# V differences of the prompt attention: formed by the projection stage and kept in DRAM, or formed in the attention from two loads per key block

## The chip, the cores and the metric

The kernel is one program on one core of a Trainium2 chip. The metric is device time in microseconds (us), the median of several executions. Names of engines are those of the profile: PE is the matmul engine (PEld its weight loads), DVE the vector engine, ACT the scalar engine, POOL the GpSimd engine, and SP the queue from which this kernel issues its DMAs. Each engine, and SP too, works its own instructions in the order in which they are written, so a waiting instruction holds up all that stand behind it there.

## The reference, cut to what matters

Two layers (DEPTH = 2) are applied to a prompt of 2048 tokens and to 8 short sample sequences. In each layer one projection gives u, z_s, q, k, v and z_a; u goes through a state-space branch (SSM), q, k and v through a stick-breaking attention of 8 heads of 64; both results are gated, joined, and sent through an output projection onto the residual. What the change touches is the prompt attention:

```
z = einsum('bqhd,bkhd->bhqk', q, k) * HEAD_DIM ** -0.5      # 2048 x 2048 for each head
mask = k_pos < q_pos                                        # strictly causal
after = exclusive sum, from the right, of -softplus(z)
a = exp(log_sigmoid(z) + after) where mask, else 0
o = einsum('bhqk,bkhd->bqhd', a, v)
```

With u[s] the product of sigmoid(-z) over the keys from s up to the query, a[s] is the difference of two neighbouring u. The sum over a[s] v[s] can therefore be written with u[s] and with differences of neighbouring rows of V. The kernel does that: it never forms a, and it multiplies u by (V[s-1] - V[s]), with V[-1] = 0, and adds one row of V for each query at the end.

## The kernel before

Work is laid out in tiles of 128 tokens. `project` makes one of the six column groups for half of the tiles: for the group v it takes, for each tile, 24 matmuls (L673 to L675) into a PSUM tile pm (two buffers), an ACT copy into an SBUF tile kn (L760, three buffers), a store of it to the output and one to the DRAM tensor v_d. Then it reads the same tile back from v_d, shifted by one row, into an x2 tile (two buffers, shared with other uses and shown as x by the profile), subtracts on POOL (L771), and stores the result to a second DRAM tensor, dv_d:

```
dv = e2("x2", [128, 512], bufs=2)
self.dma(dv, self.v_d[l][i * 128 - 1:i * 128 + 127, :])
gp.tensor_sub(dv, dv, cp)
self.dma(self.dv_d[l][i * 128:(i + 1) * 128, :], dv)
```

This happens 32 times: for 16 prompt tiles in each of two layers, eight at a time in four v stages. In the trace these stages lie at about 310 to 402 us, 840 to 900, 1718 to 1800 and 2313 to 2368.

`attn_prompt` loops over blocks of up to four query tiles (t0, nt), pairs of heads (hp) and key blocks of 512 (kc), from the last to the first. One turn of the kc loop is called a unit here; there are 96, 40 in layer 0 and 56 in layer 1. A unit loads a tile V1 (named V in the profile; two buffers) from dv_d, and K; PE multiplies Q and K into pz (L819, L820), ACT takes the sigmoid (L824), DVE runs the product along the keys (a scan, L826, tile u), PE transposes u in blocks (L836, tile pt), DVE copies one head's block to SBUF (L838, tile aT) and ACT the other's (L839), and PE multiplies aT by V1 into po (L842). At the end of a head pair DVE adds the row of V and multiplies by the gate (L851). The prompt attention of layer 0 runs from about 1025 to 1920 us, with the layer's output projection and the first half of the next layer's input projection in between; that of layer 1 from about 2480 to the end.

Beside the first v stage (320 to 400 us) runs a part of `ssm_mats(1)`: powers of the state matrix, a chain of DVE instructions (L444, L446, L447, L449, tiles T and t) each of which needs a POOL instruction (L445, L448), then sines and cosines on ACT (L414, L415) and products on DVE and POOL (L416 to L419). The next weights are split into a high part wH on ACT and a low part wL by `split` (L171, L172), for every second of them on POOL.

The order on each engine isn't written out by hand: the program is built with a scheduler that puts all instructions in order by a time model of its own, so an edit in one place can move instructions of others.

## Time and profile before

| | us |
|---|---|
| median of 3 runs | 3268.61 |
| lowest and highest of them | 3263.90 and 3268.92 |
| the profiled execution | 3266.1 |
| its span, first to last instruction | 3264.3 |
| PE busy | 3019.6 (93%) |
| DVE busy | 2228.8 (68%) |
| ACT busy | 1297.2 (40%) |
| POOL busy | 715.0 (22%), 468 instructions |
| mean granted clock of PE, 1 is full | 0.971 |

The table is read so: PE works in 93% of the span, so what remains are about 245 us in which it waits, and some stretches in which its clock is lowered. Busy shares are means over stages with different limits; which wait ends last has to be looked up in each stage. The profiled execution lies 2.5 us under the median of the runs.

### The profile page before, as it was taken

Reading aid. Unit: us, or ns where it says so; the run is one execution under the profiler, and the core shown is the slowest. Engines: PE = TensorE matmul, PEld = TensorE weight load, DVE = VectorE, ACT = ScalarE, POOL = GpSimd, SP = SyncE. Lnnn points to the kernel's source line nnn. Section 1 sums busy time; section 2 is a strip of 40 time slices with the busy share of each in tenths; the row PEclk is TensorE's granted clock in tenths of the full one; section 3 lists DMA queues with packets and bytes.
Section 4 is the critical chain, followed back from the end, with each engine's and each line's share of the span. In section 5 each row is a group of like instructions: output and inputs, shape, how many; then the busy total and the mean of one; then the engine's idle time right before and its main releaser. Section 6 shows DMA issues by size and latency. Waiting matters only on the chain. (4 is left out here: it accounts for less than half of the span.)

```text
span 3264.3 us, 47172 instructions
## 1 busy us (share of the span) xinstructions
PE 3019.6 (93%) x16902; PEld 2241.4 (69%) x16902; DVE 2228.8 (68%) x3885; ACT 1297.2 (40%) x2646; POOL 715.0 (22%) x468
## 2 busy tenths in 40 slices
PE   6978679899998999999999999989999899999998
PEld 4756577798767667667777785757789565666665
DVE  6699785667466776677895534376583989776865
ACT  5622225334342343465443324263343345343422
POOL 1155663102211022211021002222200202111210
PEclk8989899999999999999999999999999899999999
DMA  6645654565776974343344237437853846444642
GB/s 208 164 141 176 215 166 150 146 192 167 258 241 216 315 218 151 121 139 117 113 150 153 88 104 268 142 99 216 268 177 119 259 129 200 141 128 136 203 140 73
DMA packets 516100, 555.28 MB, mean 170 GB/s; under 512 B 87203, under 2 KB 369491, under 8 KB 515098
## 3 DMA queue, kind: packets, MB, share of 16 engines
q1 hardware_dynamic: 515866, 552.26, 53.9%
q8 instruction: 134, 2.20, 0.3%
q14 instruction: 100, 0.82, 0.1%
HBM read 378.12 MB, written 169.86 MB: 168 GB/s over the span
## 5 line engine op out<-in xcount | busy, mean ns | idle before, releaser
L826 DVE TENSOR_TENSOR_SCAN u<-u 128x512 f32<-128x512 f32 (+3 forms) x640 | 722.2, 1162 | 94.2 <-ACT u L824 90.7
L673 PE MATMUL pm<-wH,hH 128*128 128x512 f32 x1088 | 448.9, 414 | 38.4 <-ACT kn L760 18.9
L675 PE MATMUL pm<-wH,hL 128*128 128x512 f32 x1088 | 446.2, 410 | 10.6 <-POOL hL L649 6.0
L674 PE MATMUL pm<-wL,hH 128*128 128x512 f32 x1088 | 444.0, 408 | 9.9 <-DVE wL L172 8.0
L839 ACT COPY aT<-pt 128x512 f32<-128x512 f32 (+1 forms) x376 | 174.9, 469 | 595.3 <-PE pt L836 569.1
L836 PEld LDWEIGHTS pt<-ident,u 128*128 128x128 f32 x2176 | 242.1, 142 | 230.8 <-issue 194.1
L824 ACT ACTIVATE u<-pz 128x512 f32<-128x512 f32 (+3 forms) x640 | 320.7, 535 | 177.1 <-PE pz L822 61.3
L838 DVE COPY aT<-pt 128x512 f32<-128x512 f32 (+1 forms) x376 | 199.4, 533 | 253.8 <-PE pt L836 242.3
L836 PE MATMUL pt<-ident,u 128*128 128x128 f32 x2176 | 352.0, 285 | 12.9 <-DVE aT L838 9.3
L842 PE MATMUL po<-aT,V 128*64 128x512 f32 (+1 forms) x1504 | 317.7, 505 | 16.0 <-DVE aT L838 8.1
L819 PE MATMUL pz<-K,Q 128*128 128x512 f32 (+2 forms) x640 | 272.9, 427 | 6.1 <-ACT u L824 1.8
L726 PE MATMUL pm<-hH,wH 128*128 128x384 f32 (+1 forms) x768 | 258.9, 337 | 18.4 <-DVE kn L731 18.4
L673 PEld LDWEIGHTS pm<-wH,hH 128*128 128x128 f32 x1088 | 210.0, 193 | 90.2 <-ACT kn L760 20.4
L728 PE MATMUL pm<-hH,wL 128*128 128x384 f32 (+1 forms) x768 | 257.4, 336 | 10.2 <-POOL wL L172 10.2
L172 POOL TENSOR_TENSOR wL<-wr,wH 128x512 fp32r<-128x512 f32 x96 | 152.1, 1595 | 498.2 <-ACT wH L171 326.8
L727 PE MATMUL pm<-hL,wH 128*128 128x384 f32 (+1 forms) x768 | 257.8, 336 | 0.0
L675 PEld LDWEIGHTS pm<-wH,hL 128*128 128x128 f32 x1088 | 210.2, 193 | 66.2 <-POOL hL L649 10.6
L674 PEld LDWEIGHTS pm<-wL,hH 128*128 128x128 f32 x1088 | 210.2, 193 | 58.8 <-DVE wL L172 11.3
L820 PE MATMUL pz<-K,Q 128*128 128x512 f32 (+2 forms) x640 | 236.3, 370 | 0.0
L1241 PE MATMUL pm<-owH,mH 128*128 128x512 f32 x512 | 205.0, 402 | 2.1 <-ACT mH L171 1.2
L1242 PE MATMUL pm<-owL,mH 128*128 128x512 f32 x512 | 204.1, 399 | 3.1 <-DVE owL L172 3.1
L1243 PE MATMUL pm<-owH,mL 128*128 128x512 f32 x512 | 202.4, 396 | 0.0
(373 smaller groups left out, 5252.0 us busy)
## 6 DMA issues: line engine op xcount, KB each, us to landing
wr<-in_w_in_dram SPq DMA_DIRECT2D x192, 256.0 KB
K<-kT SPq DMA_DIRECT2D x184, 256.0 KB
Q<-qT SPq DMA_DIRECT2D x112, 256.0 KB
wm<-in_w_mod_dram SPq DMA_DIRECT2D x24, 1024.0 KB
V<-dv_d SPq DMA_DIRECT2D x92, 256.0 KB
out_dram<-kn SPq DMA_DIRECT2D x68, 256.0 KB
qT<-x SPq DMA_DIRECT2D x64, 256.0 KB
kT<-x SPq DMA_DIRECT2D x64, 256.0 KB
```

The costliest lines, as they stand in the source:

```text
L673: pe.matmul(ps, hH[:, k, cs], wH[k], start=k == 0, stop=False)
L674: pe.matmul(ps, hH[:, k, cs], wL[k], start=False, stop=False)
L675: pe.matmul(ps, hL[:, k, cs], wH[k], start=False, stop=k == KT - 1)
L726: pe.matmul(ps[:, 0:n], wH[k][:, ws], hH[:, k, 0:n], start=k == 0, stop=False)
L727: pe.matmul(ps[:, 0:n], wH[k][:, ws], hL[:, k, 0:n], start=False, stop=False)
L728: pe.matmul(ps[:, 0:n], wL[k][:, ws], hH[:, k, 0:n], start=False, stop=k == KT - 1)
L819: pe.matmul(pz[:, c0:512], Q1[:, qi], K1[:, 0:N], start=True, stop=False)
L820: pe.matmul(pz[:, c0:512], Q2[:, qi], K1[:, 0:N], start=False, stop=not diag)
L824: sc.activation(u[:, o:512], pz[:, c0:c1], AF.Sigmoid, scale=-0.125)
L826: v.tensor_tensor_scan(un, un, un, 1.0 if diag else carry[hh * 4 + i], ALU.mult, ALU.bypass)
L836: pe.transpose(pTs[hh][:, i * 128:(i + 1) * 128], As[hh][i][:, off + j * 128:off + (j + 1) * 128], ident)
L842: mm = pe.matmul(po[c, s], V1[:, j, c], aTs[hh][:, s], start=diag and j == 0, stop=kc == 0 and j == 3, tile_position=(0, hh * 64))
```

## The change

`dv_d` is gone, with the read-back, the subtraction and the store in `project`. In `attn_prompt` each unit loads the plain rows of V from v_d into V1 and the rows one above into a new tile Vp (one buffer), and POOL subtracts in place. For the first key block (kc = 0, 36 of the 96 units) the row above does not exist; there a memset and two loads stand for one.

```
--- before.py
+++ after.py
-        self.dv_d = per([SEQ, 512], F32, "dv_d")
@@ project, after the store to v_d
-                        if i < 16:
-                            dv = e2("x2", [128, 512], bufs=2)
-                            if i == 0:
-                                gp.memset(dv[0:1, :], 0.0)
-                                self.dma(dv[1:128, :], self.v_d[l][0:127, :])
-                            else:
-                                self.dma(dv, self.v_d[l][i * 128 - 1:i * 128 + 127, :])
-                            gp.tensor_sub(dv, dv, cp)
-                            self.dma(self.dv_d[l][i * 128:(i + 1) * 128, :], dv)
@@ attn_prompt, in the kc loop
                     V1 = ap.tile([128, 4, 128], F32, name="V1", bufs=2)
-                    self.dma(V1[:, 0:nk // 128], self.dv_d[l][ks, rp].rearrange("(b p) c -> p b c", p=128))
+                    Vp = ap.tile([128, 4, 128], F32, name="Vp", bufs=1)
+                    nb = nk // 128
+                    self.dma(V1[:, 0:nb], self.v_d[l][ks, rp].rearrange("(b p) c -> p b c", p=128))
+                    if kc:
+                        self.dma(Vp[:, 0:nb], self.v_d[l][kc * 512 - 1:kc * 512 + nk - 1, rp].rearrange("(b p) c -> p b c", p=128))
+                    else:
+                        gp.memset(Vp[0:1, 0, :], 0.0)
+                        self.dma(Vp[1:128, 0, :], self.v_d[l][0:127, rp])
+                        self.dma(Vp[:, 1:nb], self.v_d[l][127:nk - 1, rp].rearrange("(b p) c -> p b c", p=128))
+                    gp.tensor_sub(V1[:, 0:nb], Vp[:, 0:nb], V1[:, 0:nb])
```

Lines behind the edit in `scratch` are one lower in the changed kernel (L771 has no successor; L760 is L759, L445 is L444, L172 is L171), those in `attn_prompt` behind the new loads are one lower too.

POOL in the first v stage, before (x_3710, x_3744, x_3777 and x_3810 are the differences of the first four tiles, t and T the power chain, kn in L698 the last k tile):

```order
L445 TENSOR_TENSOR t_2345<-T 128x16x32
L771 TENSOR_TENSOR x_3710<-x_3710,kn 128x512
L445 TENSOR_TENSOR t_2408<-T 128x16x32
L448 TENSOR_TENSOR t_2345<-T 128x16x32
L698 TENSOR_TENSOR kn<-kn,kg 128x512
L771 TENSOR_TENSOR x_3744<-x_3744,kn 128x512
L448 TENSOR_TENSOR t_2408<-T 128x16x32
L445 TENSOR_TENSOR t_2345<-T 128x16x63
L771 TENSOR_TENSOR x_3777<-x_3777,kn 128x512
L445 TENSOR_TENSOR t_2408<-T 128x16x63
L448 TENSOR_TENSOR t_2345<-T 128x16x63
L771 TENSOR_TENSOR x_3810<-x_3810,kn 128x512
```

and the same place of POOL in the changed kernel:

```order
L444 TENSOR_TENSOR t_2343<-T 128x16x32
L444 TENSOR_TENSOR t_2406<-T 128x16x32
L447 TENSOR_TENSOR t_2343<-T 128x16x32
L697 TENSOR_TENSOR kn<-kn,kg 128x512
L447 TENSOR_TENSOR t_2406<-T 128x16x32
L444 TENSOR_TENSOR t_2343<-T 128x16x63
L444 TENSOR_TENSOR t_2406<-T 128x16x63
L447 TENSOR_TENSOR t_2343<-T 128x16x63
L447 TENSOR_TENSOR t_2406<-T 128x16x63
L418 TENSOR_TENSOR T<-T,t_2342 128x2048
L418 TENSOR_TENSOR T<-T,t_2405 128x2048
L171 TENSOR_TENSOR wL<-wr,wH 128x512 x4
```

The subtractions between the steps of the power chain are gone, and the first four wL now stand behind both of the large products (L418), where one of the four stood between them before.

ACT in the same stage, before (kn_3740 to kn_3905 are v tiles 2 to 7; T_2339 and T_2402 are the two layers' power tables):

```order
L760 COPY kn_3740<-pm_3715 128x512
L760 COPY kn_3773<-pm_3748 128x512
L760 COPY kn_3806<-pm_3781 128x512
L760 COPY kn_3839<-pm_3814 128x512
L414 ACTIVATE t1_2344<-T_2339 128x2048
L415 ACTIVATE t2_2345<-T_2339 128x2048
L760 COPY kn_3872<-pm_3847 128x512
L414 ACTIVATE t1_2407<-T_2402 128x2048
L415 ACTIVATE t2_2408<-T_2402 128x2048
L760 COPY kn_3905<-pm_3880 128x512
```

and in the changed kernel (kn_3733 to kn_3878 are the same tiles 2 to 7; x2_4825 and x2_4840 are parts of a later input tile):

```order
L759 COPY kn_3733<-pm_3708 128x512
L630 ACTIVATE x2_4825<-x2_4825,rs_4746 128x512
L759 COPY kn_3762<-pm_3737 128x512
L630 ACTIVATE x2_4840<-x2_4840,rs_4746 128x512
L759 COPY kn_3791<-pm_3766 128x512
L759 COPY kn_3820<-pm_3795 128x512
L413 ACTIVATE t1_2342<-T_2337 128x2048
L414 ACTIVATE t2_2343<-T_2337 128x2048
L413 ACTIVATE t1_2405<-T_2400 128x2048
L414 ACTIVATE t2_2406<-T_2400 128x2048
L759 COPY kn_3849<-pm_3824 128x512
L759 COPY kn_3878<-pm_3853 128x512
```

The copy of the sixth v tile stood behind one pair of activations (L414, L415) and stands behind both pairs now; two scalings of a later input tile (L630) have moved up between the earlier copies.

POOL in the attention of layer 0 beside the output projection, before (mL is the low part of its input, yt its result):

```order
L172 TENSOR_TENSOR mL<-m,mH 128x512
L1245 TENSOR_TENSOR yt<-yt,xt 128x512 x2
L172 TENSOR_TENSOR mL<-m,mH 128x512
L1245 TENSOR_TENSOR yt<-yt,xt 128x512 x2
L172 TENSOR_TENSOR mL<-m,mH 128x512
```

and in the changed kernel:

```order
L171 TENSOR_TENSOR mL<-m,mH 128x512
L1244 TENSOR_TENSOR yt<-yt,xt 128x512 x2
L804 TENSOR_TENSOR V_10643<-Vp,V_10643 128x512
L171 TENSOR_TENSOR mL<-m,mH 128x512
L1244 TENSOR_TENSOR yt<-yt,xt 128x512 x2
L804 TENSOR_TENSOR V_10760<-Vp,V_10760 128x512
L801 MEMSET Vp 1x128
```

One subtraction of V (L804) has come in for each unit, among what POOL did there.

## Rows read from the trace of the kernel before

**Rows 1.** The page: busy time, share of the span and instructions of each engine.

```profile
PE 3019.6 (93%) x16902; PEld 2241.4 (69%) x16902; DVE 2228.8 (68%) x3885; ACT 1297.2 (40%) x2646; POOL 715.0 (22%) x468
```

**Rows 2.** Stretches: length, busy (instructions) of PE, PEld, DVE, ACT, POOL; PEclk; DMA.

```profile
320.00:520.00 200.00, 150.60 (x796) 134.49 (x795) 150.64 (x114) 51.61 (x91) 130.11 (x56) 0.90 0.58 187
```

**Rows 3.** Waits of PE, 320 to 520 us: us in total, times, longest.

```profile
PE pm L673 <- ACT kn L760: 18.1, 2, 9.3
PE pm L726 <- DVE kn L731: 16.8, 6, 5.3
PE pm L728 <- POOL wL L172: 7.9, 2, 4.0
```

**Rows 4.** Timeline of ACT: start, us, instruction, [idle before, its releaser].

```profile
332.29 0.58 ACT L760 COPY kn<-pm 128x512 f32<-128x512 f32 x1 [15.54 <-POOL x L771]
...
356.75 1.91 ACT L414 ACTIVATE t<-T 128x2048 f32<-128x2048 f32 x1 [14.84 <-DVE T L449]
...
360.37 0.56 ACT L760 COPY kn<-pm 128x512 f32<-128x512 f32 x1
```

**Rows 5.** Timeline of POOL in the first v stage.

```profile
330.99 1.26 POOL L771 TENSOR_TENSOR x<-x,kn 128x512 f32<-128x512 f32 x1 [9.39 <-DMA x<-v_d]
...
356.29 1.56 POOL L771 TENSOR_TENSOR x<-x,kn 128x512 f32<-128x512 f32 x1 [0.63 <-DMA x<-v_d]
...
370.81 5.54 POOL L771 TENSOR_TENSOR x<-x,kn 128x512 f32<-128x512 f32 x2
376.31 2.24 POOL L172 TENSOR_TENSOR wL<-wr,wH 128x512 fp32r<-128x512 f32 x1
```

**Rows 6.** Timeline of DVE in the first v stage.

```profile
333.31 1.55 DVE L446 TENSOR_TENSOR T<-t,t 128x512 f32<-128x512 f32 x1 [8.71 <-POOL t L445]
...
353.82 5.10 DVE L449 TENSOR_TENSOR T<-t,t 128x1008 f32<-128x1008 f32 x2
```

**Rows 7.** Groups of POOL, 333 to 359 us: count, then busy us, mean ns.

```profile
L771 POOL TENSOR_TENSOR x<-x,kn 128x512 f32<-128x512 f32 x4 | 7.3, 1815 | 0.6 <-DMA x<-v_d 0.6
```

**Rows 8.** Timeline of SP in the first v stage.

```profile
353.27 0.38 SPq L163 DMA_DIRECT2D x<-v_d  x1
```

**Rows 9.** Waits of PE, 860 to 880 us (second v stage).

```profile
PE pm L674 <- POOL wL L172: 1.7, 1, 1.7
```

**Rows 10.** Waits of PE, 1700 to 1810 us (third v stage).

```profile
PE pm L728 <- POOL wL L172: 2.0, 1, 2.0
```

**Rows 11.** All subtractions of the kernel (groups of POOL): count, busy us, mean ns.

```profile
L771 POOL TENSOR_TENSOR x<-x,kn 128x512 f32<-128x512 f32 x32 | 48.3, 1513 | 164.6 <-DMA x<-v_d 119.1 <-DMA E<-mm 18.4 <-ACT wH L171 7.8
```

**Rows 12.** Stretches of the prompt attention, columns as in rows 2.

```profile
1060.00:1960.00 900.00, 885.70 (x5006) 631.70 (x5007) 607.43 (x997) 381.61 (x747) 137.78 (x90) 0.99 0.48 152
2490.00:3250.00 760.00, 720.44 (x3961) 491.36 (x3961) 561.20 (x709) 289.66 (x632) 116.05 (x68) 0.98 0.51 156
2640.00:2720.00 80.00, 78.88 (x454) 52.34 (x450) 65.95 (x91) 35.14 (x75) 0.00 (x0) 1.00 0.54 149
2720.00:3000.00 280.00, 275.25 (x1451) 182.83 (x1448) 218.49 (x261) 114.36 (x239) 53.76 (x34) 0.99 0.47 146
```

**Rows 13.** Groups of DVE by form, 2640 to 2720 us (POOL idle).

```profile
L826 DVE TENSOR_TENSOR_SCAN u<-u 128x512 f32<-128x512 f32 x28 | 34.3, 1256 | 3.0 <-ACT u L824 2.9
```

**Rows 14.** Groups of DVE by form, 2720 to 3000 us (POOL with 34 instructions).

```profile
L826 DVE TENSOR_TENSOR_SCAN u<-u 128x512 f32<-128x512 f32 x102 | 135.6, 1364 | 14.3 <-ACT u L824 13.7
```

**Rows 15.** Waits of PE, 1060 to 1960 us.

```profile
PE pt L836 <- DVE aT L838: 4.9, 5, 2.1
```

**Rows 16.** Waits of PE, 2490 to 3250 us.

```profile
PE po L842 <- DVE aT L838: 8.1, 8, 1.8
...
PE pt L836 <- DVE aT L838: 4.5, 6, 1.5
```

**Rows 17.** Timeline near the end: a V load and the first matmul that reads it.

```profile
3194.00 0.37 SPq L163 DMA_DIRECT2D V<-dv_d  x1
...
3201.02 0.65 PE L842 MATMUL po<-aT,V 128*64 128x256 f32 x4
```

## The prediction

> **What bounds the kernel now.** The page comes first: PE is busy in 93% of the span, the next engine in 68% [rows 1]. So the time is PE's work, which this change leaves as it is, plus the waits of PE and the stretches with a lowered clock. The question is only which waits go and which come. I then looked for the stage that the removed steps touch with the most of PE's waiting in it: the 200 us from 320, in which PE is busy for 150.60 us, at a mean granted clock of 0.90 [rows 2]. The waits of that stretch name the v copies: two waits of 18.1 us in total before a first v matmul, for the ACT copy L760; 7.9 us for wL from POOL; and 16.8 us for DVE, later, in the za and zs groups [rows 3]. The reader is to see there that the removed steps are near all three: POOL does L771 and wL, and the copy waits for what POOL does.
>
> **The first v stage, step by step.** POOL's first L771 starts at 330.99, after 9.39 us of idling for its read-back [rows 5]. Three things hang on it. The ACT copy at 332.29 needs the kn buffer that this subtraction reads, so it waits 15.54 us in its queue, and PE behind it 9.3 us [rows 3, 4]. The power chain has its next POOL step right behind the L771, so DVE idles 8.71 us, to 333.31 [rows 6]. And everything behind on POOL starts later. Between 333 and 359 POOL then runs four more L771, 7.3 us in all [rows 7]; at the 1.26 us that one takes undisturbed [rows 5] that is 5.0 us of POOL work that the chain's steps share the engine with.
>
> The second wait of PE has another cause: the copy at 360.37 stands in ACT's queue behind a pair of activations that waited 14.84 us for the power chain on DVE [rows 4]. So PE's second wait ends when the chain ends, and the chain's last steps run from 353.82 to 358.92 [rows 6]. Without the 8.71 us and without the 5.0 us the chain ends 13.7 us earlier, at about 345.2. The new order of ACT takes some back: the copy that PE waits for there, that of the sixth tile, now stands behind both pairs of activations, not one, that is behind two more of 1.9 us each [rows 4]. The last pair can start when the chain ends and takes 3.8 us, so the copy starts at about 349.0 where it started at 360.37: 11.4 us sooner. PE is there earlier (the first wait is gone, or shrinks to the load that the moved-up scalings wait for) and waits for it all the same: what is late next is the chain, as before, only sooner.
>
> Then the weights: the first wL started at 376.31, behind two L771 of 5.54 us together [rows 5]. In the new order those are gone, but the second large product comes ahead of all four wL. As that product follows DVE's part of the chain, I move it by the chain's 11 to 14 us and let the two orders cancel. I take **-12 us** for this stage. The ends: if the new order of ACT and POOL costs what the L771 gave, only the 3.9 us over from 5.0 + 8.71 after 9.8 us of later steps is left, so -4; if both copy waits and both wL waits go whole, 18.1 + 7.9 = -26 [rows 3]. I take the value nearest to the DVE row, because the chain is what ends last in this stretch.
>
> **The other v stages.** In them PE waits little, and only a wL that stands behind an L771 on POOL reaches it: 1.7 us in the second and 2.0 us in the third [rows 9, 10]; I found none in the fourth. Ends 0 and -3.7 us; taken: **-3 us**. The 32 stores to dv_d, the 32 read-backs and two memsets leave SP and POOL there and are otherwise hidden beside PE work.
>
> **What the attention gains in work.** 96 subtractions (92 of 128x512, four of half that), 36 memsets, 132 loads into Vp in place of no load (the 96 loads of V1 stay, with v_d as their source). A subtraction of 128x512 took 1.513 us in the mean and 1.26 undisturbed [rows 5, 11], so POOL gains 96 x 1.5 = 144 us in the attention and loses 48.3 in the v stages. POOL is 22% busy [rows 1], and in the attention 137.78 us of 900 and 116.05 of 760 [rows 12], so POOL itself doesn't become the bound. What is queued behind a V subtraction there is mL, yt, wL, hL and kn of the neighbouring stages; who waits for those is PE's output and projection matmuls, which run a tile or more behind.
>
> **The cost on DVE.** In 80 us of attention in which POOL did nothing a full scan took 1256 ns [rows 12, 13]; in 280 us with 34 POOL instructions it took 1364 [rows 12, 14]. 102 scans x 0.108 = 11.0 us over 34 instructions is 0.32 us of DVE time for each POOL instruction, for full scans alone. So 96 subtractions cost DVE some 31 us, perhaps 50 with the smaller forms. DVE has the room: 607.43 of 900 us, 561.20 of 760, and in the tightest stretch, where POOL was silent, 65.95 of 80 [rows 12]. That stretch holds about six units; six subtractions of 1.5 us, even if DVE stood through all of them, make 75 of 80. What reaches PE is read from PE's waits for DVE's copy aT: 4.9 us in 900 us with 90 POOL instructions, 12.6 in 760 us with 68 [rows 12, 15, 16]. Were all of these waits POOL's doing, one POOL instruction would cost PE 0.05 us in layer 0 and 0.19 in layer 1: 40 x 0.05 + 56 x 0.19 = 12.6 us. That is the upper end as long as the waits grow in proportion; the lower end is 0, because a DVE that has slack can hide all of it. A gain is excluded there: nothing is taken from DVE in the attention. Taken: half, **+6 us**.
>
> The Trainium skill's page SBUF — State Buffer (section Who interferes with whom) has a harsher rule: GpSimd and a DVE instruction with two SBUF inputs use one port pair under an exclusive lock, and the second to come blocks fully. The lengthened scans here agree in sign, at 0.108 us a scan in the mean; by the rule a subtraction could hold DVE for its whole length, 96 x 1.26 = 121 us of DVE time, as an estimate.
>
> **Is V there in time?** Before, the tightest use is at the end: a V load issued at 3194.00 is first read at 3201.02, 7.0 us later [rows 17]. Now load, second load and subtraction stand in a row. The read-back issued at 353.27 was there at 356.29, 3.0 us [rows 5, 8]; with 0.4 us for one more issue and a subtraction of 1.3 to 1.8 us that is 4.7 to 5.2 us, under 7.0. Elsewhere the load goes out a unit ahead. Vp has one buffer, so its next load waits for the subtraction before it, which is a whole unit earlier; behind it in SP's queue stand the K loads, which lose an issue of 0.4 us or two. If that cover fails, for loads slowed by others, I allow 1 us in some eight short units at the end: ends 0 and +8, taken **+1 us**.
>
> **The sum.** -12 - 3 + 6 + 1 = -8 us, on an execution of 3266.1 us, so 3258. That execution lies 2.5 us under the median of 3268.6; on the median it makes 3260.6, and I predict **3260 us**. A measurement of this kernel can tell about 0.2%, 6.5 us, from no change.
>
> **Rivals.** First, the whole stage moves up. The later waits of 16.8 us for DVE and 7.9 for wL [rows 3] belong to the same chain of powers and weights; if the loads behind the removed stores on SP go out earlier as well, all of the first stage's -26 comes, the attention hides everything, and the time is 3268.6 - 26 - 3 + 2 = 3242. For it: DVE, POOL and PE all have idle time in these 200 us [rows 2]. Against it: the chain on DVE remains and PE still waits for it.
>
> Second, the wait is only replaced. The sixth copy behind both pairs of activations, the wL behind both products, and the scalings that wait for a load in the middle of the copies give the stage -4; with 3 us from the other stages and +6 the time is 3267, no change that can be seen. For it: the order of ACT and POOL as it now stands. Against it: the 8.71 us on DVE have no other cause than the L771.
>
> Third, slower: the lock of POOL and DVE reaches PE. The place is where PE has least to hide behind, the attention of layer 1; the price is 0.5 us of DVE time for each of 96 subtractions, 48 us, and it decides once more than about a third of this comes through, because 16 us are then lost against the 15 gained. At half it is +24, and 3268.6 - 15 + 24 = 3278. This is the way in which the page's rule would come out. For it: PE's waits for aT in layer 1 are there already [rows 16]. Against it: 68 POOL instructions make at most 12.6 us of them.
>
> **Chances.** The forecast with its own range of 3251 to 3266: 0.48. All of the stage moves up: 0.14. Replaced: 0.20. Slower: 0.18. Faster by over 0.2% means under 3262: three quarters of the forecast's case and the first rival, 0.50. Slower means over 3275: 0.18. The rest, 0.32, is the same. The range for 8 in 10 leaves out half of the first rival's case and a share of the last one's: 3243 to 3279.
>
> **What would show it.** In the changed profile: DVE's idle of 8.7 us in the first v stage gone, the chain's last L449 (then L448) 12 to 15 us sooner, PE's waits for the v copy from 18.1 to about 9 to 12 us, the za group starting about 12 us sooner. No wL behind a DMA wait in the other v stages. In the attention, scans of 1.3 to 1.45 us in the mean, PE's waits for aT at 17 to 30 us in both layers together, and few or no waits of PE for V's subtraction. I am wrong if the first stage ends less than 5 us sooner, if PE waits for V1, or if PE's waits for aT double.

## The result, and the profile after

The changed kernel takes 3281.93 us, median of four runs (3278.70 to 3283.98), beside 3266.26 for the kernel before in the same comparison (3259.15 to 3268.92). The ratio is 1.0051, with a 95% interval of 1.0031 to 1.0070: slower, by about 17 us. The prediction said 3260, faster, with a range up to 3279, so both its direction and its range were wrong. The kernel after is called *after* below.

The page of after, with the same columns as [rows 1]: the instructions of PE are the same in number, and it is busy for 11 us more.

```profile
PE 3030.6 (92%) x16902; PEld 2249.6 (69%) x16902; DVE 2273.5 (69%) x3885; ACT 1298.5 (40%) x2646; POOL 820.1 (25%) x566
```

Stretches of after, to be read against [rows 2, 12]. In the first v stage PE does 162.33 us of work where it did 150.60: the gain is there. In the attention of layer 1 it does 709.18 of 760 where it did 720.44: the loss is there.

```profile
320.00:520.00 200.00, 162.33 (x882) 146.50 (x881) 143.83 (x122) 54.28 (x96) 113.06 (x48) 0.88 0.53 169
1060.00:1960.00 900.00, 884.00 (x4977) 631.41 (x4977) 635.39 (x985) 378.76 (x742) 181.21 (x133) 0.99 0.50 157
2490.00:3250.00 760.00, 709.18 (x3866) 480.95 (x3865) 583.50 (x703) 288.11 (x626) 211.25 (x141) 0.97 0.57 173
```

Matching the same matmuls in the two traces says it more closely, as far as their orders agree. In after they stand 12 us earlier at 340 us, 8 to 12 earlier up to 700, and 12 to 13 at 880; then the lead shrinks to some 6 or 7 at 1040 and 2 to 4 at 1200. It is 6 to 7 from 2640 to 2720 and 8 at 2900; at 3060 it is lost, and at the end they stand 13 us later. So the gain came, at its place and about in its size, and the attention lost some 26 us.

Waits of PE in after, first v stage (320 to 520 us), against [rows 3]: one wait of 12.0 for the v copy instead of two with 18.1, and less for DVE and wL.

```profile
PE pm L672 <- ACT kn L759: 12.0, 1, 12.0
PE pm L725 <- DVE kn L730: 10.2, 3, 5.1
...
PE pm L727 <- POOL wL L171: 5.6, 2, 4.0
```

Waits of PE in after, from 1010 to 3280 us. For aT it waits 36.9 us in all, where before it was 17.4 (9.3 and 8.1). Before, it waits 1.7 for K, and for V not at all. More than half of the growth for aT comes with the new order alone: e6 below, which has this order and no subtraction, waits 28.7.

```profile
PE pt L835 <- DVE aT L837: 24.1, 16, 3.9
PE po L841 <- DVE aT L837: 12.8, 7, 5.4
PE pz L818 <- DMA K<-kT: 7.5, 4, 2.5
PE po L841 <- POOL V L804: 5.6, 2, 4.1
```

Waits of SP's queue in after, 1010 to 3340 us. Neither of the two releasers exists before: SP now waits 195 us for them, for the subtraction that reads Vp and for the memset that precedes the paired loads. These waits take the place of others: all waits of SP in this stretch add up to 1539 us, where before they were 1629. What grew is the time of SP's issues, from 630 to 746 us, 107 of it for the 132 loads into Vp.

```profile
SPq L162 <- POOL V L804: 133.0, 49, 8.5
...
SPq L162 <- POOL Vp L801: 62.3, 24, 9.3
```

### The profile page after: what moved, and what is told of

Same layout as the page of the kernel before. It is cut to its first block, busy times and chain, and to the rows that moved or that the text cites. A ratio compares the mean times of both kernels' runs of the same rounds, so it can differ in the third digit from the quotient of the medians.

```text
span 3276.9 us, 47479 instructions
## 1 busy us (share of the span) xinstructions
PE 3030.6 (92%) x16902; PEld 2249.6 (69%) x16902; DVE 2273.5 (69%) x3885; ACT 1298.5 (40%) x2646; POOL 820.1 (25%) x566
## 3 DMA queue, kind: packets, MB, share of 16 engines
q1 hardware_dynamic: 556346, 560.11, 54.7%
## 4 chain that ended last, share of the span: by engine, by line
PE 71%; DVE 15%; DMA 6%; issue 4%; ACT 2%; SPq 1%; POOL 0%; DVEq 0%; ACTq 0%; POOLq 0%
PE po L841 8%; PE pt L835 8%; PE pm L674 5%; PE pm L673 5%; PE pm L672 5%; PE pz L818 4%; PE pm L1240 3%; PE pm L1241 3%; PE pm L1242 3%; PE pm L727 3%; PE pm L725 3%; PE pm L726 3%; PE pz L819 3%; DVE u L825 2%; PE pz L890 1%
## 5 line engine op out<-in xcount | busy, mean ns | idle before, releaser
L825 DVE TENSOR_TENSOR_SCAN u<-u 128x512 f32<-128x512 f32 (+3 forms) x640 | 764.7, 1227 | 101.5 <-ACT u L823 97.5
L804 POOL TENSOR_TENSOR V<-Vp,V 128x512 f32<-128x512 f32 (+1 forms) x96 | 148.3, 1545 | 768.1 <-DMA V<-v_d 460.7
L171 POOL TENSOR_TENSOR wL<-wr,wH 128x512 fp32r<-128x512 f32 x96 | 154.8, 1625 | 404.9 <-ACT wH L170 319.7
```

The lines of the kernel that those rows point to most:

```text
L825: v.tensor_tensor_scan(un, un, un, 1.0 if diag else carry[hh * 4 + i], ALU.mult, ALU.bypass)
```

## Experiments

Two questions had to be told apart. One: is the loss the new work (subtractions on POOL beside DVE's scans: the third rival), or the new loads in SP's queue, or only another order of instructions? Two: is there a form of it that keeps the gain?

The scheduler reorders the program on each edit, so kernels marked *kept order* build the program twice: once without the difference, to get an order, and once with it, where order-only edges hold the shared instructions of each engine and of SP to that order. Only the added instructions find their own place. Some kernels leave the differencing out (e1, e3, e4, e6) or take wrong rows for it (e12), so they are good for their time only.

```
got = program(False, None)[3]              # without the difference: its order
nc, arrays, O, _ = program(True, got)      # with it, held to that order
```

All results as ratios to the kernel before, each measured beside it; 0.001 is 3.3 us. Clock is the median of the mean granted clocks of the runs; before has 0.971 to 0.972. Of the times expected below, five came true (e7, e14, e16, e17 and e18). The other thirteen runs lie outside all the ranges given for them: e1 below, e4, e6, e9 and e12 between two ranges, the rest above.

| kernel | median us | ratio [95%] | clock |
|---|---|---|---|
| e1 no difference anywhere | 3244.94 | 0.9953 [0.9940, 0.9966] | 0.971 |
| e6 the same, in after's order | 3252.24 | 0.9970 [0.9958, 0.9983] | 0.973 |
| e4 e1 and a subtraction nobody reads | 3255.78 | 0.9981 [0.9972, 0.9991] | 0.971 |
| e9 after, kept order, second load issued by POOL | 3270.73 | 1.0024 [1.0013, 1.0035] | 0.970 |
| after | 3281.93 | 1.0051 [1.0031, 1.0070] | 0.968 |
| e17 e5, second load at once behind the first | 3278.99 | 1.0066 [1.0050, 1.0082] | 0.967 |
| e5 after, kept order | 3290.87 | 1.0091 [1.0077, 1.0106] | 0.966 |
| e7 e5, subtraction on DVE | 3295.17 | 1.0103 [1.0085, 1.0121] | 0.968 |
| e12 e5, a quarter of the data in one load | 3276.82 | 1.0045 [1.0028, 1.0062] | 0.969 |
| e13 e5, a row of zeros ahead of V | 3297.37 | 1.0107 [1.0090, 1.0124] | 0.965 |
| e15 e13, second load issued by POOL | 3278.52 | 1.0046 [1.0031, 1.0061] | 0.969 |
| e16 e13 in its own order | 3282.75 | 1.0058 [1.0041, 1.0074] | 0.970 |
| e2 after, and the old steps too | 3306.59 | 1.0145 [1.0128, 1.0162] | 0.967 |
| e3 after without the subtraction | 3343.37 | 1.0249 [1.0234, 1.0264] | 0.960 |
| e10 after with two Vp buffers | 3352.07 | 1.0274 [1.0253, 1.0294] | 0.963 |
| e8 difference after the projection | 3329.42 | 1.0212 [1.0198, 1.0227] | 0.963 |
| e11 before, first subtractions later | 3269.10 | 1.0023 [1.0009, 1.0037] | 0.970 |
| e14 difference by adding DMAs | 3267.28 | 1.0012 [1.0000, 1.0023] | 0.973 |
| e18 the same, first v stage alone | 3262.81 | 1.0016 [1.0002, 1.0030] | 0.971 |

### The removal alone (e1, e6)

e1 is before without the marked steps, with V1 loaded plain; e6 is the same work held to the order that after has.

```
-                        if i < 16:
-                            dv = e2("x2", [128, 512], bufs=2)
...
-                    self.dma(V1[:, 0:nk // 128], self.dv_d[l][ks, rp]...)
+                    self.dma(V1[:, 0:nb], self.v_d[l][ks, rp]...)
```

> The removal alone: the projection makes no differences, the attention loads V1 from v_d and multiplies by the plain rows; no Vp, no subtraction (so the output lacks the differencing). If the traces are read rightly, the removal gives its 12 to 14 us in the first v stage and nothing takes them back: 3250 to 3256 us. If the loss lies in the first half of the program or in a worse order of everything, it stays above 3265.

> The mirror: no difference at all (V1 is read plainly, so the output lacks it; no Vp, no subtraction), but all engines held to the order of the changed kernel. Theory A: 3262-3272 us, the order alone loses 17-27 us against the 3245 us of the removal in its own order. Theory B: 3243-3250 us, the order is harmless.

The removal is worth 0.47%, 15 us (e1), which is the -12 and -3 of the sum. After's order costs some 5 us of it (e6 against e1, with an uncertainty as large). So the gain was as predicted and something in the attention took twice as much. e6 against after is the cleanest pair: the same order, and only the loads and subtractions between them. By the ratios they lie 0.81% apart, 26 us; the profiled spans are 3246.9 and 3276.9. The page of e6:

```profile
PE 3015.7 (93%) x16902; PEld 2241.1 (69%) x16902; DVE 2225.9 (69%) x3885; ACT 1299.3 (40%) x2646; POOL 661.0 (20%) x434
```

PE does the same 16902 instructions in 3015.7 us and in 3030.6. So half of these 30 us is waiting and half is slower matmuls; the mean granted clock is 0.973 in e6 and 0.969 in after, and 0.004 of 3277 us is 13 us. Waits of PE for aT in e6, 1010 to 3280 us:

```profile
PE pt L840 <- DVE aT L842: 20.6, 15, 3.4
...
PE po L846 <- DVE aT L842: 8.1, 9, 1.8
```

Matched matmul by matmul, the two traces stand together until 1000 us; after is 9 us behind at 1096, 12 at 1960, 14 at 2480, 12 at 2700, 18 at 2760, 25 at 3060 and 30 at the end. Three of the steps can be read.

**At 1012 us**, where the attention begins. Timeline of after (start, us, instruction): the first K loads stand behind two Vp loads, whose issue takes 4.25 us (0.31 for the first and 3.90 for the second), and PE waits for K.

```profile
1011.92 0.51 SPq L162 DMA_DIRECT2D V<-v_d  x1
...
1012.53 4.25 SPq L162 DMA_DIRECT2D Vp<-v_d  x2
...
1016.82 1.50 SPq L162 DMA_DIRECT2D K<-kT  x2
...
1021.76 0.39 PE L818 MATMUL pz<-K,Q 128*128 128x256 f32 x1 [2.53 <-DMA K<-kT]
```

In e6 the K loads go out at 1012.11:

```profile
1011.61 0.45 SPq L166 DMA_DIRECT2D V<-v_d  x1
1012.11 0.99 SPq L166 DMA_DIRECT2D K<-kT  x2
```

The stretch from 1010 to 1050 in after, then in e6 (columns as in [rows 2]): with that wait and one of 3.0 us at 1032, the granted clock is 0.91, where e6 has 1.00.

```profile
1010.00:1050.00 40.00, 34.08 (x173) 28.84 (x171) 21.59 (x28) 12.32 (x26) 5.42 (x6) 0.91 0.71 211
```

```profile
1010.00:1050.00 40.00, 39.39 (x232) 31.65 (x230) 29.90 (x44) 16.97 (x38) 2.22 (x1) 1.00 0.81 242
```

**At 2710 us.** Timeline of after, in the order of the events: a subtraction ends at 2711.6; the Vp load that waits for it stands in SP's queue ahead of the weight loads owr, which go out at 2712.60; ACT waits 5.96 for owr with the sigmoids behind it; DVE's scan then waits 6.28 for a sigmoid, and PE 2.89, and 1.93 more for aT.

```profile
2709.65 1.95 POOL L804 TENSOR_TENSOR V<-Vp,V 128x512 f32<-128x512 f32 x1 [14.83 <-DMA V<-v_d]
2711.63 0.37 SPq L162 DMA_DIRECT2D Vp<-v_d  x1
2712.09 0.46 SPq L162 DMA_DIRECT2D K<-kT  x1
2712.60 1.84 SPq L162 DMA_DIRECT2D owr<-in_w_out_dram  x4
...
2718.07 0.62 ACT L170 CAST owH<-owr 128x512 fp32r<-128x512 f32 x1 [5.96 <-DMA owr<-in_w_out_dram]
...
2719.21 1.91 DVE L825 TENSOR_TENSOR_SCAN u<-u 128x512 f32<-128x512 f32 x1 [6.28 <-ACT u L823]
2719.23 0.50 PE L818 MATMUL pz<-K,Q 128*128 128x512 f32 x1 [2.89 <-ACT u L823]
...
2723.39 1.33 PE L835 MATMUL pt<-ident,u 128*128 128x128 f32 x5 [1.93 <-DVE aT L837]
```

In e6 the four owr loads go out at 2697.11, in a trace that is some 12 us ahead there, so in after they are 3.5 us late; ACT's wait for them in e6 is 1.55. The granted clock from 2640 to 2760 us is 0.96 in after and 1.00 in e6. There PE has waits too, five of 0.7 to 1.8 us between 2705 and 2728, and keeps its clock; in after the longest is 3.7.

**At 3062 us.** Timeline of after: the loads of V and Vp have long been issued (3044.93 and 3050.00), but the subtraction stands on POOL behind a yt that waits for DVE, so PE waits 4.10 for V, an in-order queue again, this time POOL's.

```profile
3059.53 1.26 POOL L1244 TENSOR_TENSOR yt<-yt,xt 128x512 f32<-128x512 f32 x1 [6.39 <-DVE yt L1243]
3060.75 1.26 POOL L804 TENSOR_TENSOR V<-Vp,V 128x512 f32<-128x512 f32 x1
...
3062.07 0.69 PE L841 MATMUL po<-aT,V 128*64 128x256 f32 x2 [4.10 <-POOL V L804]
```

### The work on POOL, apart from everything else (e4, e7)

e4 is e1 with one subtraction for each unit into a tile that nobody reads; e7 is e5 with the subtraction on DVE.

```
+                    Vs = ap.tile([128, 4, 128], F32, name="Vs", bufs=1)
+                    gp.tensor_sub(Vs[:, 0:nb], V1[:, 0:nb], V1[:, 0:nb])
```

> As e1, with one POOL subtraction for each unit that reads V1 and writes a tile that nobody reads: the same POOL work, which PE never waits for, without the second load (the output lacks the differencing). Theory lock: 12 to 20 us above e1, 3265 to 3275, with scans at 1.35 to 1.42 us in layer 1. Theory late V, and theory loads: within 4 us of e1.

> As the changed kernel in the kept order, but DVE subtracts instead of POOL: no POOL work beside the scans, 92 subtractions of about 0.7 us more on DVE. If POOL's work beside the scans is what costs in the kept order (11 us by the subtraction whose result nobody reads), this takes 5-12 us off the kernel that subtracts on POOL in the same order, at 3245-3253 us under theory A. If what costs is that V comes late, or DVE's own time, it is the same or slower by up to 10 us.

e4 is 0.28%, 9 us, above e1 (4 to 14 by the two intervals), with PE's order unchanged; that lies between what the two theories expected. PE's waits for aT rise from 18.5 to 24.5 us. Groups in e4, then the scans in e1 (count, busy us, mean ns): 121.1 us of subtractions make the scans 31.6 us longer, which is 0.33 us of DVE for each.

```profile
L819 DVE TENSOR_TENSOR_SCAN u<-u 128x512 f32<-128x512 f32 (+3 forms) x640 | 750.4, 1206 | 94.7 <-ACT u L817 91.5
...
L798 POOL TENSOR_TENSOR Vs<-V 128x512 f32<-128x512 f32 (+1 forms) x96 | 121.1, 1261 | 766.8 <-DMA V<-v_d 744.8
```

```profile
L817 DVE TENSOR_TENSOR_SCAN u<-u 128x512 f32<-128x512 f32 (+3 forms) x640 | 718.8, 1157 | 97.2 <-ACT u L815 93.7
```

e7 has no subtraction on POOL, its scans take 1165 ns in the mean, and it is not faster than e5 (1.0103 against 1.0091): PE then waits 12.1 us for V from DVE. So POOL's work beside the scans has its price, about 9 us, but it is not the bulk of the 32 us from e1 to after.

### Order or queue (e5, e9, e17)

e5 is after with kept order. In e9 POOL issues the second loads. In e17 SP issues them at most two places behind the first.

```
-    self.own(self.dma(Vp[:, 0:nb], ...))
+    self.own(gp.dma_start(Vp[:, 0:nb], ...))        # e9
+    tc.add_manual_dep(<SP's instruction after the first load>, second, ...)   # e17
```

> The changed kernel's own work (two loads, subtraction on POOL), but PE, DVE, ACT, and the shared instructions of POOL and SP, are held to the order that the scheduler gives the program without the difference (in the attention that is the order of the kernel before). Theory A, the scheduler's new order of the attention costs most: the time falls from 3282 us to 3253-3262 us, that is the removal's 3245 plus the 11 us of the subtraction. Theory B, the loads and the late V themselves cost it, whatever the order: 3277-3288 us, with PE's waits for aT still near 37 us.

> As the changed kernel in the kept order (3291 us), but the second load of each unit is issued by POOL from its own queue instead of SP: SP has nothing more to do in the attention than without the difference. If the loss is SP's queue, that is the second load waiting for its buffer with K's loads and the weights behind it, 3252-3265 us (the removal's 3245, and 11 us for the subtraction). If it is the moved data, or V that comes late for PE whoever issues it, 3280-3300 us.

> As the changed kernel in the kept order (3291 us), but on SP's queue no second load stands more than two issues behind its first; in the kept order it stood up to 13 behind, in one unit with four loads of weights between them (first load issued at 1127.1 us, second at 1137.3, subtraction at 1147.4, PE waited 3.6 us). If V that comes late because its second load stands behind others is the larger part of SP's 20 us, 3268-3280 us; if it is the time that second loads take from K's and the weights' loads behind them, 3284-3298 us.

The theory that the scheduler's reordering was to blame falls: with the order kept, the time is longer, 1.0091, a little above what theory B expected. PE's waits for aT are 24.0 us there, not the 37 that theory B named. After's own order gives 13 us back. A place in e5, SP's queue first: the second load of a unit stands behind four weight loads whose issue takes 9.62 us, and itself takes 3.30.

```profile
1127.14 0.39 SPq L166 DMA_DIRECT2D V<-v_d  x1
1127.62 9.62 SPq L166 DMA_DIRECT2D wm<-in_w_mod_dram  x4
1137.33 3.30 SPq L166 DMA_DIRECT2D Vp<-v_d  x1
```

POOL's subtraction in e5 starts 10 us after that load, and PE waits for it:

```profile
1147.42 1.26 POOL L809 TENSOR_TENSOR V<-Vp,V 128x512 f32<-128x512 f32 x1 [23.68 <-DMA V<-v_d]
```

```profile
1148.74 1.97 PE L846 MATMUL po<-aT,V 128*64 128x512 f32 x4 [3.55 <-POOL V L809]
```

The row of the subtraction names the load of V, issued at 1127.14, as its last releaser. That Vp's load decided is seen in e17: there the Vp load goes out ahead of the four weight loads, the subtraction starts 7.8 us behind it, at 1132.60, and PE doesn't wait.

Taking the second loads out of SP's queue (e9) gives 0.67%, 22 us, although POOL is then busier. In the matched traces, which have the same order of PE, e5 falls behind e9 by 9 us from 1010 to 1030, by 6 at 1140 and by 6 to 7 from 3000 to 3050; from 1150 to 2900 the distance stays between 19 and 23. So the price is paid at a few places, not at each of SP's waits. The pages of e5, then e9: PE's same work takes 3035.2 and 3015.1. Over all their runs the median clock is 0.966 and 0.970. e9's profiled execution (3262.0) is the shortest of its twelve, so the sizes are taken from the ratios.

```profile
PE 3035.2 (92%) x16902; PEld 2251.9 (68%) x16902; DVE 2259.3 (69%) x3885; ACT 1298.5 (39%) x2646; POOL 814.1 (25%) x566
```

```profile
PE 3015.1 (92%) x16902; PEld 2239.6 (69%) x16902; DVE 2273.3 (70%) x3885; ACT 1299.1 (40%) x2646; POOL 906.9 (28%) x698
```

e9 changes more than the issuing engine. The loads that POOL issues go through a DMA queue of their own, and the same 24.63 MB move in 8128 packets there, where on SP's queue they were 49664 (556346 less 506682). The DMA engines' share of time is no smaller: 54.6% in e5, 52.4 and 2.6 in e9. DMA queues of e5, then e9 (packets, MB, share of 16 engines):

```profile
q1 hardware_dynamic: 556346, 560.11, 54.6%
```

```profile
q1 hardware_dynamic: 506682, 535.48, 52.4%
q0 software_dynamic: 8128, 24.63, 2.6%
```

So e9 shows what it costs that SP issues these loads, and not yet why. Issuing them early on SP (e17) gives 0.25%, 8 us, hardly more than the noise; in the matched traces 6 of them come at the one place above. So about a third of the queue's cost is that the second load goes out late; the rest stays as long as SP issues it.

### How much each load costs (e12, e13, e15, e16)

e12 loads 128 rows, in one DMA, for every unit, and subtracts them from all four blocks. e13 keeps V in DRAM behind a row of zeros, so that the first key block needs no memset and one load instead of two; e15 issues that load from POOL; e16 is e13's edit with the scheduler's own order.

```
+    Vp = ap.tile([128, 128], F32, name="Vp", bufs=1)                    # e12
+    self.own(self.dma(Vp, self.v_d[l][lo:lo + 128, rp]))
+    self.own(self.dma(Vp[:, 0:nb], self.v_d[l][kc * 512:kc * 512 + nk, rp]...))   # e13, row 0 is zero
```

> As the changed kernel in the kept order, but the second load brings 128 rows of 512 B a unit instead of 512 rows, as one DMA, and the subtraction takes them for every block (the difference is wrong): SP issues and waits nearly as often, but a quarter of the data moves, and there is no POOL zeroing. If data is what costs, a large part of the loss goes: 3252-3268 us. If the waits in SP's queue and on POOL cost it, 3278-3292 us.

> As the changed kernel in the kept order (3291 us), with V in DRAM behind one row of zeros: the shifted rows of a unit at keys 0 come by one load, and the 36 pairs of loads and their 36 zeroings on POOL fall away; the data and the other 60 second loads stay as they are. In the changed kernel a pair takes SP 2.4 us from the first issue to the end of the second (84 us for 35 pairs; 4 us for those at the start of a layer's attention), against 1.0 us for a single second load. If SP held by the pairs is the larger part, 3266-3278 us; if the moved data or the subtraction is, 3285-3293 us.

> Padded as in e13 and issued from POOL as in e9: one second load a unit, from POOL's queue. If SP's queue is the whole of the loss beside the subtraction, as e4, 3253-3260 us; if something else of the loads (their data, V that waits on POOL) stays, 3262-3272 us.

> The changed kernel with the row of zeros, in the order that the scheduler gives it. If the pairs cost what e13's theory says, 8 to 18 us below the changed kernel, 3264-3274 us; if not, 3278-3290 us.

The 36 extra issues and memsets cost nothing that can be seen: e13 is no faster than e5, and e16 (1.0058) no faster than after (1.0051). Yet the pairs hold most of SP's time for Vp. Issues of Vp in after (count, then min, median and max in ns):

```profile
L162 SPq DMA_DIRECT2D Vp<-v_d x132: 241/371/5509, 1012.5 to 3242.8; - x132
```

The second issue of a pair, behind the load of 127 rows, takes 1.30 us in the median and 72.6 us in all 36; the 60 single ones take 0.41 each in the mean, not the 1.0 of the expectation. In e13 SP's time for Vp is 41 us instead of 107, and no time is gained. What the row of zeros itself costs was not run, so a gain may be hidden by it: e15, with fewer issues on POOL, lies 0.22% above e9. Against e13, e15 repeats the step from SP to POOL: 0.61%, 20 us.

The data does count: e12 differs from e13 by the bytes of the second load, and by the row of zeros, and is 0.62%, 20 us, faster (against e5, without that row too, 15). SP's waits for POOL's subtractions are as long in both (144.7 us in 76 waits, and 147.2 in 70), and so are SP's issues of Vp (37 and 41 us). So neither SP's waiting nor the time of its issues sets the price alone; the bytes do, when SP issues them. That the loads behind them land later would fit, but these profiles show no landing of SP's loads, so how the 22 us come about stays open.

### The other pieces (e2, e3, e10)

e2 keeps the old steps beside after's; e3 has after's loads without the subtraction; e10 gives Vp a second buffer.

```
-                    gp.tensor_sub(V1[:, 0:nb], Vp[:, 0:nb], V1[:, 0:nb])     # e3
-                    Vp = ap.tile([128, 4, 128], F32, name="Vp", bufs=1)      # e10
+                    Vp = ap.tile([128, 4, 128], F32, name="Vp", bufs=2)
```

> The addition alone: the projection still makes and stores its differences (which nobody reads), the attention makes them again as in the changed kernel. If the attention costs what the shift of PE between the traces shows (about 26 us from 1020 us to the end), 3287 to 3296 us. If most of the loss is an accident of the new order, 3270 to 3280.

> The changed kernel without its subtraction: V1 and Vp are loaded, nothing reads Vp, the matmuls take plain V (the output lacks the differencing). Theory lock (POOL's subtraction holds up DVE, and PE waits for DVE's copies): within 4 us of e1, 3250 to 3259. Theory loads (the second load delays the K and V loads on SP and on the DMA engines): 15 us or more above e1, 3267 to 3275. Theory late V (PE waits for the subtraction): as e1.

> The changed kernel with two buffers for Vp instead of one, in the order that the scheduler gives it: a second load waits no longer for the subtraction just before. If the single buffer is what holds SP up, 3255-3272 us; if not, as the changed kernel, 3277-3290 us.

All three came out slower than after, in orders of their own. e2 lies 0.94% above after, where e1 says that the old steps cost 0.47%: pieces with their own orders don't add. In e3, with no subtraction, SP's queue waits for the previous load into the one Vp, and PE for K. SP's and PE's waits in e3, 1010 to 3340 us:

```profile
SPq L162 <- DMA Vp<-v_d: 181.2, 78, 5.6
```

```profile
PE pz L817 <- DMA K<-kT: 37.1, 11, 12.7
```

That is the queue's cost without any work on POOL, but in another order, so it bounds nothing. e10 says nothing about the buffer: at nearly half of the places in PE's order another instruction stands than in after.

### Looking for a better place (e8, e11, e14, e18)

e8 forms the difference after the projection, through SP and POOL; e11 leaves it where it was and moves the eight subtractions of the first v stage behind the power chain; e14 stores -V to dv_d from ACT and adds the shifted V by a DMA that POOL issues; e18 does that for the first v stage alone, with the adding later. All four are in kept order.

```
+    self.own(self.dma(vp, self.v_d[l][i * 128 - 1:i * 128 + 127, c0:c1]))       # e8, in three column pieces
+    self.own(self.late(gp.tensor_sub(vp, vp, vi)))
+    tc.add_manual_dep(sub.ins, self.power.ins.name, ...)                        # e11
+    sc.activation(nv, cp, AF.Copy, scale=-1.0)                                  # e14, e18
+    gp.dma_start(dv_d[l][a:(i + 1) * 128, :], v_d[l][a - 1:i * 128 + 127, :], accum_op=ALU.add, ...)
```

> The difference stays in the projection stage and in DRAM, as before, but is taken at the end of the projection from two loads of V in pieces of 192 and 128 columns, behind the power chain on POOL; attention reads the finished difference, and all engines are held to the order without it. If the wait at the first v stage was all that the old place cost, 3246-3254 us, below both kernels. If its DMAs hold up the weights on SP's queue, 3260-3275 us.

> The kernel before, PE, DVE and ACT held to its own order; the one change is POOL's order: the eight subtractions of the first v stage stand behind the power chain instead of among its steps. If the 9.4 us wait for the read-back amid the chain is what the old place costs, and its removal gives what the whole removal gave at that place (11 to 13 us), 3249-3257 us. If the wait only moves to the V buffers or the weights' splits behind the chain, 3259-3266 us.

> The difference is taken in the projection stage, but by no engine: ACT also stores V negated, and POOL issues DMAs that add the shifted V to it in DRAM, in the first stage behind all splits of the weights; attention reads the finished difference with one load as before, and no subtraction is left. If what costs in the old place is that POOL and the V buffers wait for the read-back, it gives most of the removal's gain: 3246-3255 us, below both kernels. If ACT's second copy (32 of about 0.7 us, behind the copy for which PE waits) or POOL's issues cost as much, 3258-3268 us.

> The kernel before but for the first v stage: there ACT stores V negated too, and POOL adds the shifted V to it by DMAs issued much later, one each between the short memsets of the sample attention; all other v stages as before. If the 12 us that e14 had at 320-440 us and lost again behind its eight adding DMAs at 454 us can be kept, 3249-3257 us, below the kernel before; if something else takes them, 3259-3268 us.

None beats the kernel before. e8 is some 38 us behind already at 1000 us; its pieces go through SP's queue, which up to then waits 59.3 us for their subtractions and 40.5 for their stores, but that this is the cause is argued and not shown. In e11 the ACT copies wait for subtractions as long as before (19.1 us against 20.4, now behind the chain), and 28.9 for the store that frees their buffer, where before it was 5.0. ACT's waits in e11, 300 to 420 us:

```profile
ACT kn L764 <- DMA out_dram<-kn: 28.9, 3, 18.9
ACT kn L764 <- POOL x L775: 19.1, 3, 10.0
```

e14 is some 11 us ahead at 440 us, 6 at 520 and level at 700. POOL's row shows one possible cause, the issues of eight adding DMAs with the work of the stage behind them; they overlap, and the next instruction of POOL starts at 458.80, 5.2 us after the first. The row shows seven of them:

```profile
453.60 7.44 POOL L779 DMA_DIRECT2D dv_d<-v_d  x7
```

e18 avoids that, and its profiled execution has a span of 3250.0, 14 us under that of before. But its twelve runs go from 3251.8 to 3275.1 and their median shows no gain. The profiled execution is the fastest of the twelve, and that of before (3266.1) is slower than most of its runs, so the difference of the two spans is no gain.

## Why the prediction was wrong, step by step

The steps from e1 to after, by the ratios: removal -15; subtractions on POOL beside the scans +9 (e4 against e1); the second load by POOL's queue, with 95 us of issues on POOL, +14 (e9 against e4, not divided further; PE waits only 1.2 us for V there); issuing it from SP instead +22 (e5 against e9); the scheduler's own order -13 (after against e5). Each has an uncertainty of 4 to 8 us; together +17, which is the result by construction. In after's own order the subtractions and loads together cost 26 us (after against e6), where the prediction had +6 and +1.

**The first v stage, -12: right.** The chain's last two L448 in after run from 343.37 to 345.7, which ends 13.2 us before [rows 6]; 13.7 was predicted. DVE's timeline of after:

```profile
343.37 2.31 DVE L448 TENSOR_TENSOR T<-t,t 128x1008 f32<-128x1008 f32 x2
```

ACT's timeline of after shows what took the next place, as foreseen: the copies behind both pairs of activations. They start at 351.81, 8.6 us before [rows 4] instead of the predicted 11.4, since all four activations, not two, wait for the chain's end. PE's wait of 12.0 is at the end of the forecast 9 to 12. (The lower end of this term, -4, rests on 9.8 us of later steps for which the prediction names no row.) How much of the lead lasts to the attention is less sure: in e1's trace it is 11 us at 340 us, 2 at 1000 and 10 at 1040.

```profile
344.60 1.91 ACT L413 ACTIVATE t<-T 128x2048 f32<-128x2048 f32 x1 [14.84 <-DVE T L448]
...
351.81 1.05 ACT L759 COPY kn<-pm 128x512 f32<-128x512 f32 x2
```

**The other v stages, -3: right** within what e1 can tell (15 us in all, 11 to 20 by its interval). The two waits of PE behind it [rows 9, 10] are gone in after.

**The cost on DVE, +6: right within the noise.** The scans take 1418 ns in the stretch of [rows 14] and 1381 in that of [rows 13], inside the forecast 1.3 to 1.45. Of DVE's time a subtraction costs 0.33 us in e4, where 0.32 was predicted; PE's waits for aT grow by 6.0 us there, and the time by 9, with 4 to 14 for its bounds. PE's waits for aT did double in after, which the prediction had named as what would prove it wrong, but 11.3 of the 19.5 us are there in e6 too, without a subtraction: the new order brings them. The Trainium skill's page SBUF — State Buffer (section Who interferes with whom) lets the second of the two engines block fully, which would have been up to 121 us of DVE, as an estimate; the trace does not bear that size out, with 31.6 us for 121.1 us of subtractions in e4. The sum does not need that page.

**"Is V there in time?", +1: this is the step that failed.** It followed one V tile from its load to its matmul and found 2 us of slack, and that part nearly held: PE waits for V twice in after, 5.6 us. What failed is the price of the second load for all else that SP issues. The prediction let the K loads behind it lose "an issue of 0.4 us or two", and named nothing else. The runs put it at 22 us in the kept order (e5 against e9), and at 20 with the row of zeros (e13 against e15); after's order gives some of this back. What stands behind is not K alone but owr too, at 2712 us, with ACT's sigmoids and DVE's scans in turn behind it. SP's waits don't explain the size, as they replace others, and the time of its issues doesn't either (e13); the bytes that the loads move count (e12). By what path these reach PE is seen at the places above and open for the rest. A further 14 us come with the second load whoever issues it (e9 against e4), which the prediction had at nothing.

**A term that was missing: the clock.** The sum counted waits, and no slower matmuls after them. In after against e6 half of the loss is PE's own work, 3030.6 against 3015.7 us, and the granted clock accounts for some 13 of these 15 us.

**The rivals.** The first (whole stage up, attention hides everything) and the second (wait only replaced) didn't happen. The third named a time near the result, 3278, but by a mechanism that e4 and e7 hold to about 9 us, so that is luck; the prediction gave no chance to SP's queue as a cause of a slower kernel.

## What to carry to other kernels

A load added to a queue that many other loads share is not priced by its own issue, nor by the arrival of its one tile: ask which loads stand behind it, and who waits for those. Read a queue's waits against its waits without the change; 195 us of new waits meant no more waiting in all. Moving the same loads to another queue is a cheap experiment, worth 20 to 22 us here. When work moves from a stage where PE waits anyway into one where PE is 95 to 98% busy, count each longer wait of PE twice, once as a wait and once for the granted clock after it, as half of the loss was each here, until a row shows otherwise. An edit in a scheduled program is best judged with the order held, in both directions, before anything is said about the parts.

## What the runs showed of the hardware

- Waits of PE of 2.5 and 3.0 us in otherwise dense work were followed by a lower granted clock, between the two levels of 1.2 and 2.4 GHz: 0.91 in the mean over 1010 to 1050 us in after, against 1.00 in e6. Five waits of 0.7 to 1.8 us between 2705 and 2728 us in e6 left it at 1.00. Some 13 of the 30 us between the two profiles came by the clock.
- The time of a DMA issue on SP is not fixed. In after, the issue behind a Vp load of 127 rows takes 1.30 us in the median and up to 5.5; 58 of the 60 single Vp loads take under 1 us. Without such pairs (e13) 94 of 96 do.
- The same 24.63 MB cost 20 to 22 us more when SP issued the loads than when POOL did, with 49664 packets on SP's queue and 8128 on POOL's (e5 and e9).
- 121.1 us of subtractions on POOL made DVE's scans 31.6 us longer (e4 against e1).
- The issue of an adding DMA from DRAM to DRAM takes POOL 1.02 us in the median of 32; eight in a row delayed the next instruction by 5.2 us (e14).
